# A hybrid convolution, expert and mLSTM block on one core: moving the column sums that open the convolution's layer norm further down TensorE's order

## The chip, the cores and the metric

The kernel runs on one core of a Trainium2 chip. The metric is the device time of one execution in microseconds (us), as the median of several runs. One execution was also taken with the hardware profiler; all rows below come from it.

## What is computed

The program is a first block (a convolution branch and a spatial gating branch, mixed by gates, then a mixture of 32 experts) followed by two layers of a second block. Only the convolution branch and what runs beside it matter here. For 512 tokens and 1024 channels, cut from the reference:

```python
def layer_norm(x, g, b):
    mu = jnp.mean(xf, axis=-1, keepdims=True)
    var = jnp.mean(jnp.square(xf - mu), axis=-1, keepdims=True)
    y = (xf - mu) * lax.rsqrt(var + EPS)
    return (y * g + b)
def conformer_conv_branch(a, conv_w, conv_b, ln_g, ln_b, w_o, b_o):
    a1, a2 = jnp.split(a, 2, axis=-1)
    a = a1 * jax.nn.sigmoid(a2)
    y = lax.conv_general_dilated(a, kern, ...) + conv_b     # 31 taps, depthwise
    y = jax.nn.silu(layer_norm(y, ln_g, ln_b))
    return y @ w_o + b_o
    ...
    g_a, g_b = jnp.split(jax.nn.sigmoid(gate_logits), 2, axis=-1)
    x = x + (g_a * y_a + g_b * y_b) @ w_out[l] + b_out[l]   # y_a convolution, y_b spatial gating
```

## The kernel before

Channels lie on the 128 partitions, tokens along the free axis, so a 1024 x 512 tensor is eight tiles of 128 x 512. A layer norm over channels needs sums across partitions. These are made on TensorE: `colsum` multiplies 128-token pieces of a tile by a column of ones (four instructions in the program, eight in the trace, since each float32 one runs as two), and `bcast_t` spreads a per-token number back over the partitions by four transposes (`bc` tiles).

Dense products run in three float16 products per 128 x 128 weight block (`mm3`): high part of the weights times high part of the data, high times low, low times high. One k-step below means these three matmuls of 128x512; an output tile (an `m`) takes eight k-steps and goes to one of eight PSUM tiles `p`. The weights come in chunks of 1 MB. A chunk is loaded into a `w` tile by a DMA from SP's queue, ScalarE makes the high half `wh` (L276), VectorE the low half `wl` (L280). A chunk of the products named below serves two output tiles.

The products of the first block run in this order on TensorE: `wa` (convolution input), `wv`, `wu`, `wgb`, `wga` (gates), `wsgo` (spatial gating output, data tiles `sh`), `wco` (convolution output, data tiles `ch`), `wo`, then routing and the experts.

Beside them the convolution runs in the background as `fillers`: the even channel tiles tap by tap on VectorE (L646), the odd ones as a scaled copy on ScalarE (`tap`, L628) and an add on GpSimd (L629). When a channel tile is whole, `conv_done` adds it to `ya` on GpSimd (L613, L615). With the last one it queues the norm's four steps: `ln_mu` (column sums `cs` of `ya`, mean `mu` on VectorE, L578), `ln_sub` (spread the mean, subtract it on VectorE, L587, squares on ScalarE, sums of squares `lsq` on VectorE, L465), `ln_r` (column sums of `lsq`, inverse root `rs`), `ln_out` (spread it, scale on VectorE, L602, SiLU and high half `ch` on ScalarE, L603 and L604, low half on VectorE, L606).

Every engine runs its own instructions in the order in which the program issued them. That order is set at build time by a clock of the builder, `self.clk`: each matmul adds its nominal length (0.213 us for a 128x512 one). `self.at(delay, fn)` puts a step into a heap with the due time `clk + delay`; `poll`, called after every k-step, issues the steps that are due. So a step lands behind a counted number of matmuls, whether or not its data are ready when the chip gets there, and each of the norm's steps queues the next by a delay of its own (3.0, 14.0 and 4.0).

Of the kernel before, what the change touches and what calls it, by code (L numbers as in the profile page):

```python
# [120 lines left out]
class Net:  # L121
# [385 lines left out]
    def first_mixer(self):  # L507
# [102 lines left out]
        def conv_done(m):  # L610
            whole.append(m)
            if len(whole) == 2:
                nc.gpsimd.tensor_add(ya, yc[whole[0]], yc[whole[1]])  # L613
            elif len(whole) > 2:
                nc.gpsimd.tensor_add(ya, ya, yc[m])  # L615
            if len(whole) == KD:
                self.at(5.0, ln_mu)

        def conv(m, ap):
            b = v("conv_b")[:, m:m + 1]  # L620
            yc[m] = self.t2([P, T], s="yc")
            if m % 2:
                y = yc[m]

                def tap(j):
                    q = self.tapp.tile([P, T], F32, name=self.name("tap"), tag="tap")
                    d = CONVW - 1 - j
                    nc.scalar.activation(q[:, d:T], ap[:, 0:T - d], AF.Copy, scale=cw[:, j, m:m + 1])  # L628
                    nc.gpsimd.tensor_add(y[:, d:T], y[:, d:T], q[:, d:T])  # L629
                    if j == 0:  # L630
                        conv_done(m)

                self.fillers[1].append(lambda: nc.scalar.activation(
                    y, ap, AF.Identity, scale=cw[:, CONVW - 1, m:m + 1], bias=b))
                for j in reversed(range(CONVW - 1)):
                    self.fillers[1].append(lambda j=j: tap(j))
                return
# [14 lines left out]
            def done():  # L652
                nc.scalar.activation(yc[m], y[0], AF.Copy)
                conv_done(m)
# [1101 lines left out]
```

## Time and profile before

| | |
|---|---|
| median of 3 runs | 1986.64 us (1985.33 to 1991.63) |
| the profiled execution | 1986.07 us |
| its span, first to last instruction | 1984.4 us |
| TensorE busy | 1923.0 us (97%) |
| VectorE, ScalarE, GpSimd busy | 989.8, 715.0, 239.4 us |
| mean granted TensorE clock | 0.989 |

Busy time counts instructions in flight, so a busy TensorE is not one at its peak, and its clock is granted in two levels, full (1.00, 2.4 GHz) and half (0.50, 1.2 GHz). What can be saved is seen where TensorE waits or runs at the lower level.

### The profile page before, as it was taken

How to read it: one execution, taken by the hardware profiler on the slowest of the kernel's cores; microseconds unless marked ns; L12 is line 12 of the kernel's file. 1: busy time of each engine (PE TensorE's matmuls, PEld its weight loads, DVE VectorE, ACT ScalarE, POOL GpSimd, SP SyncE). 2: the span in 40 equal slices, each digit the busy share in tenths (PEclk: the TensorE clock that was granted, in tenths of full speed). 3: DMA queues.
4: the chain of work that ended last, by engine and by line, in shares of the span. 5: the costliest groups of instructions: out<-in, count | busy, mean ns of one | idle time of the engine just before them, and what ended most of it. 6: DMA issues, size and time to landing. Idle time of an engine off the chain costs nothing.

```text
span 1984.4 us, 26464 instructions
## 1 busy us (share of the span) xinstructions
PE 1923.0 (97%) x10925; PEld 984.9 (50%) x10926; DVE 989.8 (50%) x1515; ACT 715.0 (36%) x1026; POOL 239.4 (12%) x194
## 2 busy tenths in 40 slices
PE   8999979989999999998999999999999999999997
PEld 3444434454434444433555864444485467444445
DVE  7888955642323323327645674423267558444223
ACT  6759643331111111115434564422143246443120
POOL 1998940010000000002000000000000000000000
PEclk9999989999999999998999999999999999999998
DMA  6333223369999999995421232322213322233201
GB/s 250 128 107 107 71 100 106 135 252 386 393 403 402 370 413 412 413 413 187 147 70 58 86 118 95 106 107 103 109 50 124 106 104 89 103 107 113 99 22 43
DMA packets 82476, 347.59 MB, mean 175 GB/s; under 512 B 9776, under 2 KB 12080, under 8 KB 57776
## 3 DMA queue, kind: packets, MB, share of 16 engines
q1 hardware_dynamic: 79776, 343.12, 46.4%
q10 hardware_dynamic: 2576, 2.74, 0.5%
q8 instruction: 87, 1.43, 0.3%
q14 instruction: 37, 0.30, 0.0%
HBM read 343.73 MB, written 2.10 MB: 174 GB/s over the span
## 4 chain that ended last, share of the span: by engine, by line
PE 58%; DMA 4%; DVE 3%; ACT 1%; issue 0%; POOL 0%; DVEq 0%; ACTq 0%; SPq 0%
PE p L182 48%; DMA ewl<-in_we_dram 3%; PE y L182 2%; PE pg L182 2%; PE pu L182 1%; PE sc L182 1%; PE xs L182 1%; DMA w<-in_we_dram 1%; DVE wl L280 1%; PE num L182 1%; DVE x L1266 1%; DVE d L1265 0%; PE bc L186 0%; DVE racc L465 0%; DVE xh L1234 0%
## 5 line engine op out<-in xcount | busy, mean ns | idle before, releaser
L182 PEld LDWEIGHTS <-wh 128*128 128x128 f16 x4448 | 436.3, 98 | 403.1 <-issue 9.1
L182 PE MATMUL p<-xh,wh 128*128 128x512 f16 (+1 forms) x1824 | 469.3, 347 | 3.4 <-ACT xh L1230 2.2
L280 DVE SCALAR_TENSOR_TENSOR wl<-w,wh 128x2048 f16<-128x2048 f32 x130 | 303.6, 2347 | 109.9 <-ACT wh L276 107.8
L182 PEld LDWEIGHTS <-wl 128*128 128x128 f16 x2224 | 218.2, 98 | 203.7 <-issue 4.6
L182 PE MATMUL p<-xh,wl 128*128 128x512 f16 (+1 forms) x912 | 316.7, 347 | 1.3 <-DVE wl L280 1.3
L182 PE MATMUL p<-hid,wh 128*128 128x512 f16 (+1 forms) x1152 | 308.8, 355 | 0.0
L276 ACT ACTIVATE wh<-w 128x2048 f16<-128x2048 f32 x130 | 244.9, 1902 | 6.1 <-PE p L182 3.8
L182 PE MATMUL p<-hid,wl 128*128 128x512 f16 (+1 forms) x576 | 204.7, 355 | 0.0
L629 POOL TENSOR_TENSOR yc<-yc,tap 128x511 f32<-128x511 f32 (+14 forms) x120 | 193.1, 1609 | 57.2 <-ACT tap L628 48.7
L182 PE MATMUL p<-hn,wh 128*128 128x512 f16 x576 | 173.0, 382 | 0.5 <-DVE hn L550 0.5
L465 DVE TENSOR_TENSOR pacc<-pacc,sq 128x256 f32<-128x256 f32 (+1 forms) x41 | 21.4, 522 | 208.3 <-ACT sq L464 208.2
L182 PE MATMUL p<-hn,wl 128*128 128x512 f16 x288 | 109.8, 381 | 0.0
L1610 DVE TENSOR_TENSOR relu<-relu 128x512 f32<-128x512 f32 (+1 forms) x76 | 46.1, 606 | 126.3 <-ACT hid L1609 126.3
L464 ACT ACTIVATE sq<-p 128x256 f32<-128x256 f32 (+1 forms) x41 | 18.9, 461 | 229.2 <-PE p L182 229.0
L1608 ACT ACTIVATE relu<-p 128x512 f32<-128x512 f32 (+1 forms) x76 | 39.9, 525 | 159.3 <-PE p L182 159.3
L646 DVE SCALAR_TENSOR_TENSOR yc<-ap,cw,yc 128x511 f32<-128x511 f32 (+14 forms) x120 | 88.3, 736 | 2.8
L1040 DVE TENSOR_TENSOR h<-h,pu 128x512 f32<-128x512 f32 x16 | 11.0, 688 | 154.3 <-PE pu L182 109.1
L628 ACT ACTIVATE tap<-ap,cw 128x511 f32<-128x511 f32 (+14 forms) x120 | 79.6, 701 | 22.0 <-POOL yc L629 21.9
L1039 ACT ACTIVATE h<-pg,wd 128x512 f32<-128x512 f32 x16 | 11.0, 687 | 195.3 <-PE pg L182 140.6
L182 PE MATMUL p<-wh,xh 128*128 128x512 f16 x256 | 79.7, 379 | 0.0
L1074 DVE TENSOR_TENSOR x<-x,sc 128x512 f32<-128x512 f32 x128 | 78.4, 681 | 1.6 <-PE sc L182 1.2
L1063 ACT ACTIVATE yhl<-y,wd 128x512 f16<-128x512 f32 x32 | 21.9, 687 | 144.4 <-PE y L182 116.5
(378 smaller groups left out, 2520.2 us busy)
## 6 DMA issues: line engine op xcount, KB each, us to landing
w<-in_wd_dram SPq DMA_DIRECT2D x130, 1024.0 KB, 4.9
w<-in_we_dram SPq DMA_DIRECT2D x62, 1024.0 KB, 12.6
ewh<-in_we_dram SPq DMA_DIRECT2D x90, 512.0 KB, 11.4
ewl<-in_we_dram SPq DMA_DIRECT2D x90, 512.0 KB, 10.2
ex<-in_we_dram SPq DMA_DIRECT2D x160, 256.0 KB, 5.3
x<-in_x_dram SPq DMA_DIRECT2D x8, 256.0 KB, 6.9
w<-in_wd_dram SPq DMA_DIRECT2D x4, 512.0 KB, 6.9
out_dram<-x ACTq DMA_DIRECT2D x8, 128.0 KB, 1.7
```

The lines of the kernel that those rows point to most:

```text
L182: self.nc.tensor.matmul(out, l, r, start=start, stop=stop)
L276: nc.scalar.activation(wh, t, AF.Copy, scale=WS)
L280: nc.vector.scalar_tensor_tensor(wl, t, WS, wh, op0=OP.mult, op1=OP.subtract)
L465: nc.vector.tensor_add(acc[:, s], acc[:, s], q)
L628: nc.scalar.activation(q[:, d:T], ap[:, 0:T - d], AF.Copy, scale=cw[:, j, m:m + 1])
L629: nc.gpsimd.tensor_add(y[:, d:T], y[:, d:T], q[:, d:T])
L646: V.scalar_tensor_tensor(y[0][:, d:T], ap[:, 0:T - d], cw[:, CONVW - 1 - d, m:m + 1], y[0][:, d:T], op0=OP.mult, op1=OP.add)
L1063: nc.scalar.activation(o[:, 0], y[q], AF.Copy, scale=wc)
L1074: V.tensor_add(xt[d], xt[d], ps)
L1266: (nc.gpsimd if i and last and k in (0, 2, 4) else nc.vector).tensor_add(x, x, d)
L1608: nc.scalar.activation(a, ps, AF.Relu, scale=IWS)
L1610: nc.vector.tensor_mul(a, a, a)
```

## The change

One number changes: the delay with which `conv_done` queues `ln_mu`.

```diff
             if len(whole) == KD:
-                self.at(5.0, ln_mu)
+                self.at(21.0, ln_mu)
```

Because the later steps of the norm are queued by their predecessors, they move along. No instruction is added or removed, and the numbers of instructions on all engines are the same.

TensorE, the place of the four `cs` sums that read `ya`. First the order before; the names are `p` for the output tile in PSUM, `hn` for the data of the gate products, `wh` and `wl` for the weights:

```order
L182 LDWEIGHTS wl_2013
L182 MATMUL p_2298<-hn_196,wl_2013 128x512
L182 MATMUL cs_2306<-ones_102,ya_211 128x1 x4
L182 LDWEIGHTS wh_2012
L182 MATMUL p_2298<-hn_197,wh_2012 128x512
```

They stood behind the second k-step of the sixth output tile of `wga`. The order of the change, with `sh` as the data of the spatial gating's output product:

```order
L182 LDWEIGHTS wl_2183
L182 MATMUL p_2385<-sh_1655,wl_2183 128x512
L182 MATMUL cs_2401<-ones_102,ya_211 128x1 x4
L182 LDWEIGHTS wh_2182
L182 MATMUL p_2385<-sh_1656,wh_2182 128x512
```

They now stand behind the third k-step of the first output tile of `wsgo`, that is 6 + 8 + 8 + 3 = 25 k-steps further down. The spreading of the mean follows 5 k-steps later in both, the sums of `lsq` after 22 k-steps more, the spreading of `rs` after 7 (before: 5 + 22 + 7 as well).

VectorE, between the last tap of the convolution (L646) and the first subtraction of the norm (L587). Before:

```order
L646 SCALAR_TENSOR_TENSOR yc_1826<-ap_854,cw_209,yc_1826 128x482
L280 SCALAR_TENSOR_TENSOR wl_2268<-w_400_1897,wh_2267 128x2048
L578 TENSOR_SCALAR mu_2305<-cs_2306 128x4
L587 TENSOR_TENSOR yc_405<-yc_405,bc_2327 128x512
L587 TENSOR_TENSOR yc_412<-yc_412,bc_2327 128x512
```

With the change:

```order
L646 SCALAR_TENSOR_TENSOR yc_1826<-ap_854,cw_209,yc_1826 128x482
L280 SCALAR_TENSOR_TENSOR wl_2268<-w_400_1897,wh_2267 128x2048
L280 SCALAR_TENSOR_TENSOR wl_2330<-w_427_2015,wh_2329 128x2048
L578 TENSOR_SCALAR mu_2400<-cs_2401 128x4
L280 SCALAR_TENSOR_TENSOR wl_2390<-w_441_2101,wh_2389 128x2048
L587 TENSOR_TENSOR yc_405<-yc_405,bc_2423 128x512
```

Two weight halves that stood behind the norm's subtractions now stand ahead of them, one of them ahead of the mean.

VectorE, between the last sum of squares (L465) and the first scaling of `ln_out` (L602). Before:

```order
L465 TENSOR_TENSOR lsq_2332<-lsq_2332,sq_2360 128x512
L280 SCALAR_TENSOR_TENSOR wl_2373<-w_427_2015,wh_2372 128x2048
L280 SCALAR_TENSOR_TENSOR wl_2433<-w_441_2101,wh_2432 128x2048
L436 TENSOR_SCALAR rsa_2455<-cs_2450 128x4
L442 TENSOR_TENSOR rsw_2457<-rsy_2456 128x4
L443 SCALAR_TENSOR_TENSOR rsw_2457<-rsw_2457,rsa_2455 128x4
L444 SCALAR_TENSOR_TENSOR rs_2458<-rsw_2457,rsy_2456 128x4
L773 SCALAR_TENSOR_TENSOR gate_1716<-p_2428,b_61_205,gate_1716 128x512
L602 TENSOR_TENSOR yc_405<-yc_405,bc_2495 128x512
```

With the change:

```order
L465 TENSOR_TENSOR lsq_2428<-lsq_2428,sq_2456 128x512
L773 SCALAR_TENSOR_TENSOR gate_1716<-p_2385,b_61_205,gate_1716 128x512
L773 SCALAR_TENSOR_TENSOR gate_1766<-p_2460,b_61_205,gate_1766 128x512
L280 SCALAR_TENSOR_TENSOR wl_2491<-w_455_2185,wh_2490 128x2048
L773 SCALAR_TENSOR_TENSOR gate_1835<-p_2486,b_61_205,gate_1835 128x512
L436 TENSOR_SCALAR rsa_2542<-cs_2537 128x4
L442 TENSOR_TENSOR rsw_2544<-rsy_2543 128x4
L443 SCALAR_TENSOR_TENSOR rsw_2544<-rsw_2544,rsa_2542 128x4
L444 SCALAR_TENSOR_TENSOR rs_2545<-rsw_2544,rsy_2543 128x4
L773 SCALAR_TENSOR_TENSOR gate_1884<-p_2518,b_61_205,gate_1884 128x512
L280 SCALAR_TENSOR_TENSOR wl_2563<-w_469_2270,wh_2562 128x2048
L602 TENSOR_TENSOR yc_405<-yc_405,bc_2588 128x512
```

Four evacuations of `wsgo` outputs (L773) and the two weight halves of the first `wco` chunks now lie between the two parts of the norm, where one evacuation and two `wsgo` weight halves lay.

## Rows read from the trace of the kernel before

**Rows 1.** The page: the span, busy time of each engine, and the span in 40 slices of 49.6 us (TensorE's busy tenths, its granted clock in tenths, GB/s moved by DMA).

```profile
span 1984.4 us, 26464 instructions
PE 1923.0 (97%) x10925; PEld 984.9 (50%) x10926; DVE 989.8 (50%) x1515; ACT 715.0 (36%) x1026; POOL 239.4 (12%) x194
...
PE   8999979989999999998999999999999999999997
...
PEclk9999989999999999998999999999999999999998
...
GB/s 250 128 107 107 71 100 106 135 252 386 393 403 402 370 413 412 413 413 187 147 70 58 86 118 95 106 107 103 109 50 124 106 104 89 103 107 113 99 22 43
```

**Rows 2.** TensorE's waits from 200 to 480 us, longest first: what waited, for whom, us in total, times, longest.

```profile
PE cs L182 <- POOL ya L615: 13.5, 1, 13.5
PE rk L182 <- DVE mk L933: 5.7, 1, 5.7
```

**Rows 3.** Stretches around that wait: us, busy time of each engine (instructions), granted clock, DMA share, GB/s.

```profile
250.00:255.00 5.00, 5.00 (x25) 2.25 (x23) 4.89 (x6) 2.31 (x4) 4.84 (x3) 1.00 0.22 49
...
256.00:270.00 14.00, 1.04 (x5) 1.04 (x6) 2.78 (x2) 4.05 (x5) 12.28 (x9) 0.67 0.28 101
270.00:272.00 2.00, 2.00 (x8) 1.17 (x9) 0.16 (x1) 0.00 (x0) 0.00 (x0) 0.50 0.00 0
272.00:276.00 4.00, 4.00 (x16) 1.72 (x15) 0.00 (x0) 0.00 (x0) 0.00 (x0) 0.70 0.00 0
276.00:280.00 4.00, 4.00 (x22) 1.93 (x20) 3.46 (x6) 2.07 (x4) 0.00 (x0) 1.00 0.00 0
```

**Rows 4.** TensorE in order of time around the wait: start, us from the start of the first to the end of the last, instruction, how many, idle time before and what ended it.

```profile
255.06 0.38 PE L182 MATMUL p<-hn,wl 128*128 128x512 f16 x1
268.96 1.87 PE L182 MATMUL cs<-ones,ya 128*128 128x1 f32 x8 [13.53 <-POOL ya L615]
270.69 1.01 PE L182 MATMUL p<-hn,wh 128*128 128x512 f16 x2
271.50 0.63 PE L182 MATMUL p<-hn,wl 128*128 128x512 f16 x1
...
274.06 0.55 PE L182 MATMUL p<-hn,wl 128*128 128x512 f16 x1
274.44 0.60 PE L182 MATMUL p<-hn,wh 128*128 128x512 f16 x2
...
275.52 0.38 PE L182 MATMUL p<-hn,wl 128*128 128x512 f16 x1
275.74 0.60 PE L186 MATMUL bc<-ident,mu 128*128 128x128 f32 x4
276.18 0.59 PE L182 MATMUL p<-hn,wh 128*128 128x512 f16 x2
```

**Rows 5.** TensorE in order of time where nothing holds it: the sums of `lsq`, the first matmuls behind the second spreading, and the first matmuls of `wco`.

```profile
290.21 0.38 PE L182 MATMUL p<-sh,wl 128*128 128x512 f16 x1
290.42 0.95 PE L182 MATMUL cs<-ones,lsq 128*128 128x1 f32 x8
291.23 0.38 PE L182 MATMUL p<-sh,wh 128*128 128x512 f16 x1
...
296.20 0.59 PE L182 MATMUL p<-sh,wh 128*128 128x512 f16 x2
...
329.87 0.59 PE L182 MATMUL p<-ch,wh 128*128 128x512 f16 x2
```

**Rows 6.** Who works during the wait. GpSimd's instructions by shape from 250 to 270 us (busy, mean ns), then in order of time the weight halves `wl` on VectorE, ScalarE's last instructions ahead of the norm, and GpSimd's last two adds.

```profile
L629 POOL TENSOR_TENSOR yc<-yc,tap 128x485 f32<-128x485 f32 x1 | 3.3, 3258 | 0.1
L629 POOL TENSOR_TENSOR yc<-yc,tap 128x490 f32<-128x490 f32 x1 | 3.2, 3153 | 0.1
...
L629 POOL TENSOR_TENSOR yc<-yc,tap 128x491 f32<-128x491 f32 x1 | 1.2, 1228 | 0.1
...
L629 POOL TENSOR_TENSOR yc<-yc,tap 128x484 f32<-128x484 f32 x1 | 1.2, 1202 | 0.1
...
250.02 2.78 DVE L280 SCALAR_TENSOR_TENSOR wl<-w,wh 128x2048 f16<-128x2048 f32 x1
259.04 2.29 DVE L280 SCALAR_TENSOR_TENSOR wl<-w,wh 128x2048 f16<-128x2048 f32 x1 [2.55 <-ACT wh L276]
...
257.11 1.89 ACT L276 ACTIVATE wh<-w 128x2048 f16<-128x2048 f32 x1
259.39 0.68 ACT L765 ACTIVATE gate<-p,cols 128x512 f32<-128x512 f32 x1
...
266.31 2.60 POOL L615 TENSOR_TENSOR ya<-ya,yc 128x512 f32<-128x512 f32 x2
```

**Rows 7.** VectorE in order of time through the norm: first subtraction, last sum of squares, the first of the inverse root, an evacuation of `wsgo`, first scaling, first and last low half of `ch`.

```profile
276.45 1.88 DVE L587 TENSOR_TENSOR yc<-yc,bc 128x512 f32<-128x512 f32 x3 [5.42 <-PE bc L186]
...
285.28 0.69 DVE L465 TENSOR_TENSOR lsq<-lsq,sq 128x512 f32<-128x512 f32 x1 [0.15 <-ACT sq L464]
...
292.82 0.15 DVE L436 TENSOR_SCALAR rsa<-cs 128x4 f32<-128x4 f32 x1
...
294.60 0.74 DVE L773 SCALAR_TENSOR_TENSOR gate<-p,b,gate 128x512 f32<-128x512 f32 x1
296.40 1.28 DVE L602 TENSOR_TENSOR yc<-yc,bc 128x512 f32<-128x512 f32 x2 [1.06 <-PE bc L186]
298.63 0.69 DVE L606 TENSOR_TENSOR ch<-yc,ch 128x512 f16<-128x512 f32 x1 [0.95 <-ACT ch L604]
...
308.50 0.69 DVE L606 TENSOR_TENSOR ch<-yc,ch 128x512 f16<-128x512 f32 x1 [0.68 <-ACT ch L604]
```

**Rows 8.** Behind the mixer: stretches as in rows 3 around the start of the experts and near their end, and TensorE's first expert matmuls.

```profile
420.00:430.00 10.00, 6.26 (x49) 5.08 (x48) 7.27 (x20) 6.45 (x13) 5.07 (x5) 1.00 0.65 263
430.00:440.00 10.00, 6.23 (x76) 6.03 (x78) 3.46 (x13) 1.88 (x2) 0.58 (x1) 0.66 0.01 2
440.00:450.00 10.00, 10.00 (x48) 3.31 (x46) 4.05 (x18) 1.80 (x4) 0.00 (x0) 1.00 0.70 257
...
800.00:900.00 100.00, 97.02 (x610) 41.07 (x608) 31.14 (x58) 12.53 (x20) 0.00 (x0) 1.00 1.02 413
...
439.78 1.08 PE L182 MATMUL pg<-w,xs 128*64 128x512 f32 x4
```

## The prediction

> **What bounds the kernel now.** I read the page first: TensorE is busy for 1923.0 of 1984.4 us, and the one slice of the mixer where both its busy share (7) and its granted clock (8) fall is the sixth, 248 to 298 us [rows 1]. The table of waits says why: one wait of 13.5 us of the sums `cs` for GpSimd's `ya`, the longest between 200 and 480 us, more than twice the next [rows 2]. The stretches show its second price: the clock is 0.67 on average from 256 to 270 us, 0.50 from 270 to 272, 0.70 from 272 to 276 and 1.00 afterwards [rows 3]. So TensorE comes back at half speed. The order of time gives the figures [rows 4]: a matmul starts at 255.06, then nothing until the sums at 268.96, and the matmuls behind them stand 0.43 us apart (270.69 to 271.50 for two) until 274.44, then 0.22. Meanwhile 25 k-steps of ready work stand behind the sums in TensorE's order, which nothing but the order holds back. GpSimd ends `ya` at 266.31 + 2.60 = 268.91 [rows 6]; it follows ScalarE's taps and VectorE, not TensorE.
>
> **What the change does to this wait.** First the pace. From 296.20 to 329.87 lie 52 k-steps (4 left of one `wsgo` output, six outputs of 8) with nothing between, 33.67 us [rows 5], so 0.6475 us each and 0.2158 per matmul. The sums without a wait push the next matmul from 290.21 + 0.22 to 291.23, 0.80 us; a spreading from 275.52 + 0.22 to 276.18, 0.44 us [rows 4, 5].
>
> In the new order the matmul behind 255.06 starts at 255.28. 25 k-steps take 16.19 us, so the sums are reached at 271.47, and their first weight load, which reads `ya`, at 271.26 (the sums stand 0.21 behind the last matmul's start [rows 5]). If `ya` is there, TensorE gains three terms:
> - the stall, from 255.28 to 268.96: 13.68 us;
> - the sums at the lower clock, 270.69 - 268.96 = 1.73 against 291.23 - 290.42 = 0.81: 0.92 us;
> - nine matmuls at the lower clock, 274.44 - 270.69 = 3.75 against 9 x 0.2158 = 1.94: 1.81 us.
>
> Together 16.4 us. The same from the other end: from 255.28 to the first matmul of `wco` are 86 k-steps (6 + 8 + 8 + 64), two sums and two spreadings, 55.69 + 1.60 + 0.88 = 58.2 us, so `wco` starts at 313.45 where it started at 329.87.
>
> **Is `ya` there?** This is the tight place. The work let through brings one new VectorE instruction in front of `mu`, `wl_2330`, and GpSimd slows beside such an instruction: the add of 128x485 took 3258 ns, its `wl` running from 259.04, where 128x484 took 1202; that of 128x490 took 3153 beside the `wl` from 250.02, where 128x491 took 1228 [rows 6]. That is 1.9 to 2.1 us per `wl`. When will it run? ScalarE is free at 259.39 + 0.6 = 260.0, does one gate then (its accumulator ends at 259.3) and the `wh` from about 260.6, 1.89 us; `wl_2330` runs from 262.5, in the middle of GpSimd's last taps. So `ya` ends at 268.91 + 2.0 = 270.9, at the latest bound of a whole `wl` (2.29) at 271.20, at the earliest at 268.91 if it falls between. All are before 271.26. I take no wait; the margin is 0.1 to 2.3 us, likeliest 0.3. The Trainium skill, "SBUF — State Buffer", section "Who interferes with whom", speaks against this margin: a VectorE instruction with two SBUF inputs and a GpSimd one that reads SBUF exclude each other, and whichever starts first holds the pair of ports for its whole length. By that rule the loss is the whole 2.29, the margin 0.06, and a handover would use it up; the slowed adds here lost slightly less than that.
>
> **What moves along, and why it costs nothing.** The rest of the norm hangs on TensorE's places, and these come out at the old times: spreading at 271.47 + 0.81 + 5 x 0.6475 = 275.52 (was 275.74), the sums of `lsq` at 290.2 (290.42), the second spreading at 295.6 (295.76). VectorE is ready for each. `wl_2390` waits for `wh_2389`, which follows the gate of the last `wga` output (ending at 269.7) on ScalarE and ends near 272.3, so it is done by 274.9, behind `mu` at 272.5, before the subtractions at 276.2. These run to 285.97 [rows 7]. Behind them queue evacuations and `wl_2491` (0.74 + 0.74 + 2.29 + 0.74 us): the inverse root starts near 291 instead of 292.82; an evacuation and `wl_2563` end by 296, where the scaling can start (296.40 before). So the first `ch` is whole at 299.3 and the last at 309.2, as before [rows 7]. `wco` needs the first at 313.45 and each next one 4 x 0.6475 = 2.6 us later, while they come 1.4 us apart: cover of 14.1 us, which was 30.5. The `wco` weights of the first two chunks are whole at 290 and 296, ahead of 313.45. The first `wsgo` accumulators stand full until VectorE comes to them at 286, four of the eight PSUM tiles at most; TensorE would stop only with eight. GpSimd's one instruction in the norm and SP's loads keep their order; a load waits for the `wl` that frees its tile, and none of those moves behind the matmul that needs the chunk.
>
> **Does the gain survive the experts?** From 440 us on the weights' stream runs at a DMA share of 1.0 (413 GB/s at 800 to 900 us), so this stage could take back what the mixer gives. But its loads stop for want of free tiles: 263 GB/s at 420 to 430, 2 GB/s at 430 to 440, and go on when TensorE uses the first expert weights from 439.78 [rows 8]. The stream's restart hangs on TensorE and moves with it. Even if all the loading ahead stayed at its old time, there are 10 us of rest; at most 16.4 - 10 = 6.4 us would be lost.
>
> **Sum.** The profiled execution took 1986.07 us (span 1984.4), 0.57 under the median of the runs shown. 1986.07 - 16.42 = 1969.65; with half of that 0.57 as the median's due I say 1969.9 us.
>
> **The rivals.**
> - *The sums still wait for `ya`.* For it: the margin of 0.1 to 0.3. Against: every row gives an end before 271.26. The rule above speaks for it too. If one more `wl` length (2.0) fell in, the wait is 1.7: 1971.6. If TensorE's clock fell again, add up to 0.92 + 1.81: 1974.3. The wait of 5.7 us for `mk` lies in the stretch where the clock shows 0.66, so a wait under 2 us may cost the clock or not [rows 2, 8].
> - *The experts give part back.* The loads ahead stay, up to 6.4 us lost: 1972 to 1976. Against: the rest at 430 to 440.
> - *The gain is lost whole, or the change does nothing.* The `wco` product or the experts wait for what TensorE no longer waits for: 1981 to 1988. The order shows that the sums do move past 16.2 us of work, so it must come from a wait behind.
> - *Slower: `wco` waits for `ch`.* VectorE runs in order, and `rsa`, which opens the inverse root, now stands behind three evacuations and `wl_2491`, which waits for ScalarE's `wh_2490`. If that chain slips, `ch` slips one for one. TensorE begins to pay when the first `ch` comes 14.1 us late, and the kernel is slower than before only when it comes over 14.1 + 16.4 = 30.5 us late: a slip of 35 us gives 1991. Nothing on these queues is longer than 2.3 us.
>
> **How the numbers follow.** Forecast 0.76 (own range 1968 to 1971.5), the sums wait 0.10, the experts give back 0.07, the gain lost 0.04, slower 0.03. The first three are all more than 0.3% (6 us, about what a measurement of this kernel can tell from no change) below the median. Faster 0.93, same 0.04, slower 0.03. The low end is 1969.65 less the 1.3 by which the lowest run lay under the median and 1 us for the terms' own error: 1967.3. The high end takes in the waiting sums and most of the experts' share: 1975.
>
> **What would show it.** Right: no wait of `cs` for `ya` in the table, or one under 0.5 us; a clock of 1.00 from 250 to 320 us; the first matmul on `ch` near 313.5 with no wait, the last `ch` near 309; GpSimd's last add ending near 271; the first expert matmul near 423.4; DMA still at rest just ahead of it. Wrong: a wait of `cs` over 1 us, a new wait at the head of `wco`, or expert waits for DMA that grow by more than 2 us in sum.

## The result and the profile after

The changed kernel takes 1970.36 us (median of 4 runs, 1969.88 to 1971.26), the kernel before 1988.18 us on the same footing (4 runs, 1985.33 to 1991.63). The ratio is 0.991, with a 95% interval of 0.9897 to 0.9923: faster by 0.9%. The forecast was 1969.9 us.

The profiled execution of the change took 1970.78 us. Its page, as in rows 1 (span, busy times, TensorE's busy tenths and granted clock in 40 slices):

```profile
span 1969.1 us, 26465 instructions
PE 1921.1 (98%) x10925; PEld 985.3 (50%) x10926; DVE 991.9 (50%) x1515; ACT 715.0 (36%) x1026; POOL 240.7 (12%) x194
...
PE   8999999989999999998999999999999999999997
...
PEclk9999999999999999998999999999999999999998
```

The 7 and the 8 in the sixth slice [rows 1] are nines now. TensorE's busy time fell by 1.9 us only, while the span fell by 15.3: what went is time in which it did nothing, and the little that fell is the work that ran at half speed. The table of its waits from 200 to 460 us, longest first, begins with what stood second in rows 2:

```profile
PE rk L182 <- DVE mk L933: 5.7, 1, 5.7
PE xs L182 <- DVE oh L947: 1.2, 1, 1.2
PE y L182 <- ACT hT L1048: 0.7, 1, 0.7
PE cs L182 <- ACT sq L847: 0.7, 1, 0.7
```

No wait of `cs` for `ya` is left, and no new one has come. The stretches that answer to rows 3 (busy time of TensorE, weight loads, VectorE, ScalarE, GpSimd, then granted clock, DMA share, GB/s):

```profile
255.00:270.00 15.00, 15.00 (x72) 6.81 (x70) 6.33 (x4) 7.96 (x9) 14.37 (x9) 1.00 0.51 185
270.00:272.00 2.00, 2.00 (x11) 0.92 (x10) 0.00 (x0) 1.42 (x2) 0.61 (x1) 1.00 0.00 0
272.00:276.00 4.00, 4.00 (x25) 2.33 (x23) 2.37 (x2) 1.07 (x1) 0.00 (x0) 1.00 0.00 0
```

TensorE is busy throughout and the clock stays at its full level, where it was 0.67, 0.50 and 0.70. TensorE in order of time, for rows 4 and 5: the matmul behind which the sums used to stand, the sums at their new place, and the first matmuls of `wco`:

```profile
255.92 0.38 PE L182 MATMUL p<-hn,wl 128*128 128x512 f16 x1
...
272.11 0.38 PE L182 MATMUL p<-sh,wl 128*128 128x512 f16 x1
272.33 0.95 PE L182 MATMUL cs<-ones,ya 128*128 128x1 f32 x8
...
314.31 0.59 PE L182 MATMUL p<-ch,wh 128*128 128x512 f16 x2
```

From the first of these rows to `wco` are 58.4 us; in rows 4 and 5 it was 329.87 - 255.06 = 74.8. The difference is 16.4 us, the sum that the prediction made. But the first row itself stands 0.86 us later than 255.06, and this comes from the start of the program. There, in the first product, TensorE runs at half pace until the clock rises; the row at which its matmuls become 0.22 us apart is this one in the execution before:

```profile
11.38 0.47 PE L182 MATMUL p<-xg,wl 128*128 128x512 f16 x1
11.69 0.60 PE L182 MATMUL p<-xg,wh 128*128 128x512 f16 x2
```

and this one in the execution of the change:

```profile
12.80 0.57 PE L182 MATMUL p<-xg,wl 128*128 128x512 f16 x1
13.21 0.59 PE L182 MATMUL p<-xg,wh 128*128 128x512 f16 x2
```

Nothing there was changed. By the same reading the other executions below went over between 11.0 and 13.9 us. So the two spans differ by 15.3 and not by 16.4: 0.86 us is luck of the start, and 0.2 us is spread over the rest.

### The profile page after: what moved, and what is told of

It is laid out like the page before. It is cut to its first block, busy times and chain, and to the rows that moved or that the text cites. A ratio compares the mean times of both kernels' runs of the same rounds, so it can differ in the third digit from the quotient of the medians.

```text
span 1969.1 us, 26465 instructions
## 1 busy us (share of the span) xinstructions
PE 1921.1 (98%) x10925; PEld 985.3 (50%) x10926; DVE 991.9 (50%) x1515; ACT 715.0 (36%) x1026; POOL 240.7 (12%) x194
## 4 chain that ended last, share of the span: by engine, by line
PE 54%; DMA 8%; DVE 3%; ACT 1%; issue 1%; POOL 0%; SPq 0%; DVEq 0%; ACTq 0%
PE p L182 48%; DMA ewl<-in_we_dram 5%; DMA w<-in_we_dram 3%; PE y L182 1%; PE sc L182 1%; DVE wl L280 1%; PE num L182 1%; PE xs L182 1%; PE pg L182 1%; DVE x L1266 1%; PE pu L182 0%; DVE d L1265 0%; PE bc L186 0%; DVE racc L465 0%; DVE xh L1234 0%
## 5 line engine op out<-in xcount | busy, mean ns | idle before, releaser
L465 DVE TENSOR_TENSOR pacc<-pacc,sq 128x256 f32<-128x256 f32 (+1 forms) x41 | 21.4, 521 | 208.4 <-ACT sq L464 208.3
L646 DVE SCALAR_TENSOR_TENSOR yc<-ap,cw,yc 128x511 f32<-128x511 f32 (+14 forms) x120 | 88.3, 736 | 2.8
```

The lines of the kernel that those rows point to most:

```text
L465: nc.vector.tensor_add(acc[:, s], acc[:, s], q)
L646: V.scalar_tensor_tensor(y[0][:, d:T], ap[:, 0:T - d], cw[:, CONVW - 1 - d, m:m + 1], y[0][:, d:T], op0=OP.mult, op1=OP.add)
```

## The experiments

The theory under test is that of the prediction: the whole gain is one stall of TensorE on `ya` and the half-speed clock behind it, bought out of cover that the norm had ahead of `wco`. The first four runs change the one number to other values, so each run moves the same step to another place; they share the runs of the kernel before, 1989.47 us in that comparison.

**Half of the move.**

```diff
-                self.at(21.0, ln_mu)
+                self.at(13.0, ln_mu)
```

> The sums are queued 8 builder's us later instead of 16, so 39 matmuls (8.4 us) of ready work go ahead of them instead of 75. My theory (the gain is the covered stall plus the half-speed clock behind it): TensorE reaches the sums near 263.7 to 264.6 us, ya ends near 270.6 as in the changed kernel, so 6.0 to 6.9 us of the wait stay; if a wait of that length costs the clock, up to 2.7 us more. 1976.4 to 1980. Rival (the place of the sums matters for something else, such as the order of VectorE's weight halves, and not for the wait): about 1970, as the full change, or 1988, as before.

It took 1981.65 us (ratio to the kernel before 0.9964, 0.9952 to 0.9975). TensorE in order of time:

```profile
263.06 0.38 PE L182 MATMUL p<-hn,wl 128*128 128x512 f16 x1
271.15 1.87 PE L182 MATMUL cs<-ones,ya 128*128 128x1 f32 x8 [7.71 <-POOL ya L615]
272.88 1.01 PE L182 MATMUL p<-hn,wh 128*128 128x512 f16 x2
```

The sums are reached at 263.4 and wait 7.7 us, so a part of the move gives a part of the gain and the place alone does nothing: the rival is out. The clock fell in full: the sums take 1.73 us and the next matmuls stand 0.43 us apart, as in rows 4. The time is 1.7 us above my upper end. The wait accounts for 0.8 us of this, since `ya` ends at 271.1 in this execution, not at 270.6, and TensorE comes to the sums 0.3 us before the earliest time that I had; the rest is not taken apart here.

**Three quarters of the move.**

```diff
-                self.at(21.0, ln_mu)
+                self.at(17.0, ln_mu)
```

> 57 matmuls (12.3 us) go ahead of the sums, which TensorE reaches near 267.6 to 268.5 us: a wait of 2.2 to 3.0 us for ya stays. If a wait this short keeps the clock at full speed: 1972.6 to 1973.4. If the clock falls as after the long wait: up to 2.7 us more, 1976. This prices the rival of the prediction in which the sums still wait for a short time.

It took 1975.20 us (1972.64 to 1976.88; ratio 0.9936, 0.9919 to 0.9952). The median lies nearer to the 1976 of the case in which the clock falls than to 1972.6 to 1973.4. In the profiled execution, of 1972.64 us, `ya` ended at 269.0 and the wait was short. TensorE in order of time, then two stretches of one us each with their clock:

```profile
269.02 1.05 PE L182 MATMUL cs<-ones,ya 128*128 128x1 f32 x8 [1.64 <-POOL ya L615]
269.93 0.75 PE L182 MATMUL p<-hn,wh 128*128 128x512 f16 x2
...
273.46 0.69 PE L182 MATMUL p<-sh,wh 128*128 128x512 f16 x2
```

```profile
271.00:272.00 1.00, 1.00 (x4) 0.35 (x3) 0.00 (x0) 0.00 (x0) 0.00 (x0) 0.50 0.06 16
272.00:273.00 1.00, 1.00 (x3) 0.30 (x2) 0.00 (x0) 0.00 (x0) 0.00 (x0) 0.50 0.00 0
```

A wait of 1.64 us already brings the half level, although the sums right behind it still ran at their full pace (0.91 us). Nine matmuls take 273.46 - 269.93 = 3.53 us instead of 1.94. So a short wait costs nearly as much in clock (1.6 us) as in waiting. This is the price of the rival in which the sums still wait; the 21 of the change is just beyond it.

**Further than the change.**

```diff
-                self.at(21.0, ln_mu)
+                self.at(33.0, ln_mu)
```

> The sums go 28.5 us further down than before the change, 12.3 us further than in the changed kernel, so the whole norm is later by 12.3 us: first ch near 312, last near 322, while wco starts near 314.3 and takes one more ch every 2.6 us. My theory (cover of 14.1 us at the head of wco): nothing is lost, 1970.4 within 1 us, and no wait on ch. Rival (the cover is smaller than the rows say, since evacuations and weight halves on VectorE push the norm): a wait at the head of wco, one us of time per us, 1972 to 1980.

It took 1969.87 us (ratio 0.9912, 0.9896 to 0.9929), the same as the change. The head of `wco`, in TensorE's order of time, shows no gap although the first `ch` became whole only at about 311:

```profile
312.95 0.38 PE L182 MATMUL p<-sh,wl 128*128 128x512 f16 x1
313.16 0.59 PE L182 MATMUL p<-ch,wh 128*128 128x512 f16 x2
```

So 12.3 us of the cover can be spent for nothing, and the change is on a plateau, not at a best point. No wait of the norm's sums or spreadings shows in its trace, so the edge of the cover is not seen in this run.

**Beyond the cover.**

```diff
-                self.at(21.0, ln_mu)
+                self.at(45.0, ln_mu)
```

> Beyond the cover: the sums of lsq and the second spreading now stand at the head of wco (the heap is emptied there), with the inverse root and the first scaling, SiLU and cast between them and the first ch. By the rows of the norm TensorE waits about 2.2 us for rs and 2.4 to 3.2 us for ch: 1970.4 + 4.6 to 5.4 = 1975 to 1975.8, and up to 2.7 us more if the clock falls. Rival (the wait at wco is hidden by work elsewhere, for instance taken up by the experts' loads): 1970 to 1972.

It took 1980.50 us (ratio 0.9958, 0.9942 to 0.9975): 10 us of the gain are gone. TensorE at the head of `wco`, and the stretch behind it:

```profile
312.83 0.95 PE L182 MATMUL cs<-ones,lsq 128*128 128x1 f32 x8
317.52 1.11 PE L186 MATMUL bc<-ident,rs 128*128 128x128 f32 x4 [3.74 <-DVE rs L444]
320.93 1.31 PE L182 MATMUL p<-ch,wh 128*128 128x512 f16 x2 [2.29 <-ACT ch L604]
```

```profile
320.00:326.00 6.00, 4.93 (x12) 1.65 (x12) 4.76 (x8) 5.84 (x10) 0.00 (x0) 0.50 0.00 0
```

Both waits are where the theory puts them, 6.0 us together; that for `rs` is 1.5 us longer than I had it, most of the 2.0 us by which the time lies above my upper end (1975.8 + 2.7 = 1978.5). The product then starts at a clock of 0.50: its matmuls reach from 320.9 to 365.0, 44.1 us, where they took 41.0 in the change. The first expert matmul is 9.8 us later than in the change and the end 9.7 us: the experts take up nothing of it. This is the slower rival of the prediction, made to happen; the order of the change stands 24 of the builder's us away from it.

The next three share other runs of the kernel before, 1987.58 us.

**The clock alone.** The kernel before, with dummy work ahead of the sums:

```diff
             mu = self.sm([P, NT], s="mu")
+            keep, fill = self.clk, self.ps(s="fill")
+            for j in range(60):
+                self.mm(fill, self.ones16, hn[0][:, 0], j == 0, j == 59)
+            self.clk = keep
             nc.vector.tensor_scalar(mu, self.colsum(ya), 1.0 / D, None, op0=OP.mult)
```

> The kernel before with 60 extra float16 matmuls of 128x512 (12.9 us) ahead of the sums, into a PSUM tile that nobody reads; the order of everything else is as before. The wait for ya is still there, but TensorE is busy during it. My theory (2.7 us of the 16.4 are the clock, 0.9 in the sums and 1.8 in the matmuls behind them): the sums start near 269 as before, at a granted clock of 1.00, and the time falls by 2.7 us against the kernel before. Rival (the clock costs nothing beyond the wait): same as before; or the extra matmuls outlast the wait: up to 0.5 us slower.

It took 1985.89 us; the ratio of 0.9991 (0.9981 to 1.0002) does not tell it from the kernel before. The trace does show the term. TensorE in order of time:

```profile
269.47 1.05 PE L182 MATMUL cs<-ones,ya 128*128 128x1 f32 x8 [0.52 <-POOL ya L619]
270.38 0.59 PE L182 MATMUL p<-hn,wh 128*128 128x512 f16 x2
270.81 0.38 PE L182 MATMUL p<-hn,wl 128*128 128x512 f16 x1
```

The sums take 0.91 us and the matmuls stand 0.22 us apart at once. From the start of the sums to `wco` are 327.74 - 269.47 = 58.3 us against 329.87 - 268.96 = 60.9 [rows 4, 5]: 2.6 us, where I had worked out 2.7. Half of it is not seen at the end: the span is 1983.0 us, 1.4 less than that of the execution before. `ya`, and with it the sums, come 0.5 us later in this execution, and 0.7 us is lost behind the first expert matmul, around a branch that TensorE takes in the middle of the experts (L1091, a step for overfull experts that is skipped here). The branch instruction of TensorE's queue (count, ns min/median/max, start in us) in the change and in this run, where the line number is larger by the four lines added:

```profile
L1091 PEldq COMPARE_BRANCH  x1: 445/445/445, 648.5 to 648.5; - x1
```

```profile
L1095 PEldq COMPARE_BRANCH  x1: 6009/6009/6009, 661.9 to 661.9; - x1
```

Behind it the next expert matmul waits 2.6 us instead of 0.5, and the granted clock is 0.57 from 668 to 672 us. This costs more than the 0.7 us at first; the rest is made up later among the experts. So the term is shown where it arises, and its worth in the time of the whole kernel is not.

**The cause taken away instead of the order.** The kernel before with `ya` early. This leaves out 11 of the 31 taps of one channel tile and 8 of another:

```diff
                 def tap(j):
+                    if m == 7 and 1 <= j <= 11:
+                        return
...
             def tap0(d):
+                if m == 6 and d > 22:
+                    return
```

> The order of the kernel before, but with ya ready early: the last channel tile of GpSimd's share leaves out 11 of its 31 taps and the last of VectorE's share 8 of 31, so this computes a shorter convolution for two of eight channel tiles. TensorE's order is untouched. My theory (the wait is for ya alone): ya ends near 256 to 258 us, the wait shrinks to at most 2.5 us, and the time is that of the changed kernel, 1970 to 1973. Rival (TensorE would find another wait there, such as weights or PSUM, and it is the order itself that helps): 1980 to 1988.

It took 1970.92 us (median of 5; 0.9926, 0.9902 to 0.9950), as the change does, in the old order. GpSimd's last adds and TensorE's sums:

```profile
252.51 4.53 POOL L615 TENSOR_TENSOR ya<-ya,yc 128x512 f32<-128x512 f32 x2
```

```profile
257.10 1.05 PE L182 MATMUL cs<-ones,ya 128*128 128x1 f32 x8 [0.86 <-POOL ya L615]
258.02 0.59 PE L182 MATMUL p<-hn,wh 128*128 128x512 f16 x2
258.45 0.38 PE L182 MATMUL p<-hn,wl 128*128 128x512 f16 x1
```

Where `ya` is there, the old place costs little: the wait is 0.86 us, and from the matmul ahead of the sums (255.87) to `wco` (315.38) are 59.5 us, against 74.8 in the kernel before and 58.4 in the change. The wait for `ya` is the whole cause, and the order of VectorE's weight halves, which this run leaves as it was, has no part in it. It also shows a wait of 0.86 us behind which the clock did not fall.

**The same clock term at another wait.** The changed kernel, with more of its dummy matmuls ahead of `rk`:

```diff
-    LATE, IDLE = 5, 7
+    LATE, IDLE = 5, 31
```

> The changed kernel with 31 instead of 7 of its dummy matmuls ahead of the rank sums rk in the routing, where TensorE waits 5.7 us for mk and then runs at a lower clock. 24 more matmuls are 5.2 us, inside that wait. If what the clock costs behind the sums holds there too, the 64 gather matmuls xs take about 3.7 us instead of 5.6 and the expert weights are asked for 2 us earlier: 1968.4, if the experts pass it on (the loads rest ahead of it for 8 us). Rival (the experts' weight stream takes it back): 1970.4. Other rival (the dummy matmuls end later than mk): up to 1 us slower.

It took 1972.84 us (0.9923, 0.9903 to 0.9944), 2.5 us over the change: a miss. TensorE in order of time, and three stretches with their clock:

```profile
417.24 0.19 PE L182 MATMUL rk<-mk,tri 128*128 128x32 f16 x1 [0.49 <-DVE mk L933]
418.85 5.36 PE L182 MATMUL xs<-oh,hmt 128*128 128x128 f16 x64 [1.20 <-DVE oh L947]
```

```profile
410.00:417.00 7.00, 6.75 (x32) 2.84 (x29) 6.48 (x16) 3.41 (x7) 5.24 (x5) 1.00 0.12 48
417.00:419.00 2.00, 0.57 (x13) 0.50 (x14) 1.35 (x4) 0.00 (x0) 0.00 (x0) 1.00 0.00 0
419.00:423.00 4.00, 4.00 (x49) 4.00 (x47) 0.00 (x0) 1.49 (x2) 0.00 (x0) 0.62 0.02 4
```

The wait for `mk` was filled (0.49 us, was 5.7) and the clock was full through it. It fell all the same behind the next 1.6 us, in which TensorE had ten small matmuls and a wait of 1.2 us. The gather took 5.36 us (5.68 in the change), not 3.7. And with the 48 added instructions the branch took 5987 ns, with a wait of 2.6 us behind it.

**The branch.** Two looks at what makes it slow: 8 dummy matmuls more than the change has, and 6 fewer (`IDLE` of 15 and of 1).

> The changed kernel with 15 instead of 7 dummy matmuls ahead of rk: 16 more TensorE instructions (a weight load and a matmul each), all inside the wait for mk. In the two kernels with 48 and 120 more instructions ahead of it, TensorE's branch at L1091 took 6.0 us instead of 0.45 and held the next expert matmul 2.6 us instead of 0.5. If any added instruction does that: a branch of 6 us here too and 1972.5. If it hangs on how many are added: 0.45 us and 1970.4.

> The changed kernel with 1 instead of 7 dummy matmuls ahead of rk: 12 TensorE instructions fewer. If the branch at L1091 is slow only when instructions are added: 0.45 us, and a wait of 0.5 us behind it. If the number decides in either direction: 6 us and 2.6 us may show here as well. The wait for mk grows by the 1.3 us that the dummies took and nothing else changes: 1970 to 1973 with a spread of 2 us for a single run.

With 16 instructions more the branch of the profiled execution took 445 ns, with 12 fewer 1145 ns. But the length of this record does not tell what it costs. The first expert matmul behind the branch, first with 16 more and then with 12 fewer, and a stretch with 16 more:

```profile
653.83 1.01 PE L182 MATMUL pg<-ewh,xs 128*64 128x512 f32 x1 [2.51 <-DVEq L1091]
```

```profile
652.41 0.61 PE L182 MATMUL pg<-ewh,xs 128*64 128x512 f32 x1 [0.48 <-PEq L1091]
```

```profile
653.00:657.00 4.00, 3.17 (x8) 1.31 (x9) 0.69 (x1) 0.00 (x0) 0.00 (x0) 0.57 0.99 406
```

So neither case came out as stated: with 16 more the branch is short and the wait behind it is there all the same, 2.51 us, with the lower clock behind it, as with 48 and 120 more. All three kernels with added instructions have this wait; the eight others have 0.5 us. Why is not shown. What differs in the traces is the place of the 16 KiB packets of the instruction queue q8: the last one ahead of the branch started 1.3 to 2.3 us before it in the eight kernels and 4.0 to 6.6 us before it in the three, which points to the fetching of instructions and does not show it. The times (1972.97 us, 1970.79 to 1974.87 in four runs, and 1970.88 us in one) do not tell either from the change.

## Why the prediction was right

**The stall, 13.7 us, and the clock, 0.9 + 1.8 us.** All three terms are gone from the trace of the change, and 16.4 us is what lies between the two kernels from the old place of the sums to `wco`. The runs price them apart: the filled wait gives 2.6 us for the clock between the sums and `wco`, and the run with an early `ya` gives the whole gain without moving anything.

**Whether `ya` is there.** The margin was the tight step. The one GpSimd add in the change that is slow and was not in rows 6, then the new weight half on VectorE, and GpSimd's end, for rows 6:

```profile
L629 POOL TENSOR_TENSOR yc<-yc,tap 128x483 f32<-128x483 f32 x1 | 3.1, 3131 | 0.1
...
262.74 2.84 DVE L280 SCALAR_TENSOR_TENSOR wl<-w,wh 128x2048 f16<-128x2048 f32 x1 [1.67 <-ACT wh L276]
...
268.00 2.61 POOL L615 TENSOR_TENSOR ya<-ya,yc 128x512 f32<-128x512 f32 x2
```

`wl_2330` ran at 262.74 (I had 262.5) and cost one more add its 1.9 us, as its fellows in rows 6. `ya` ended at 270.61 (I had 270.9), 1.5 us ahead of the first weight load of the sums. Of this 0.86 is the late start of TensorE, and 0.26 is that GpSimd's adds stand earlier here (from 243.26 us, in the execution before from 243.52); 0.4 is left, near the 0.3 that I called likeliest. That `wl` took 2.84 us itself where one alone takes 2.29: it began while an add was running. The Trainium skill's rule ("SBUF — State Buffer", "Who interferes with whom"), that the one which starts first keeps the other out, agrees with both rows; the add loses 1.9 us and not the whole length of the `wl`, as it began (263.52) when 2.07 us of the `wl` were left. Five more runs have the same order up to this place. In the three with other numbers of dummy matmuls the margin was 1.9 to 2.0 us; in those at 33 and 45, whose sums stand further down, it would have been 0.2 us (`ya` ended at 270.76 and 271.73, and the matmul that would have been the last ahead of the sums started at 270.96 and 271.88). So the margin moves by 2 us between executions, and it can be as thin as I feared.

**The norm keeps its times, and the cover holds.** VectorE in the change, for rows 7: first subtraction, inverse root, first scaling, first and last low half of `ch`:

```profile
277.08 1.88 DVE L587 TENSOR_TENSOR yc<-yc,bc 128x512 f32<-128x512 f32 x3 [1.40 <-PE bc L186]
...
292.04 0.16 DVE L436 TENSOR_SCALAR rsa<-cs 128x4 f32<-128x4 f32 x1 [1.27 <-PE cs L182]
...
297.03 1.28 DVE L602 TENSOR_TENSOR yc<-yc,bc 128x512 f32<-128x512 f32 x2 [0.27 <-PE bc L186]
299.26 0.69 DVE L606 TENSOR_TENSOR ch<-yc,ch 128x512 f16<-128x512 f32 x1 [0.94 <-ACT ch L604]
...
309.17 0.69 DVE L606 TENSOR_TENSOR ch<-yc,ch 128x512 f16<-128x512 f32 x1 [0.72 <-ACT ch L604]
```

With the 0.86 us of the start taken off they stand where the prediction put them, and each of the first three waits for TensorE, so nothing that was moved ahead on VectorE holds the norm up. The first `ch` is whole at 299.95, 14.4 us ahead of `wco` (I had 14.1). The runs at 33 and 45 bracket that figure: 12.3 us later costs nothing, 24 us later costs 10.

**The experts pass it on.** The first expert matmul, and the stretch ahead of it, for rows 8:

```profile
414.00:424.00 10.00, 5.79 (x71) 5.72 (x72) 3.82 (x13) 1.72 (x2) 1.02 (x1) 0.66 0.01 2
...
424.27 1.08 PE L182 MATMUL pg<-w,xs 128*64 128x512 f32 x4
```

It starts 15.5 us earlier than in rows 8, the loads rest ahead of it as before, and TensorE's waits for expert weights (`w` and `ewl`) are 2.8 and 0.6 us in all in both kernels.

**What was off.** The spread of the start, up to 2.8 us between the earliest and the latest rise of the clock in these executions, did not stand in the range. That the median of the change fell within 0.5 us of the forecast is in part luck. All terms were read from one execution of the kernel before, of 1986.07 us, while the median of that kernel moved from 1986.64 to 1988.18 with one more run and was 1987.58 to 1989.47 beside the experiments. Between the medians the change is worth 17.8 us, 1.4 more than the sum; where that difference lies, no trace here shows.

## What to carry to other kernels

A wait in front of a small instruction on an in-order engine is bought back by counting the ready work behind it: move the instruction down by at least the wait, check what comes to run beside its producer there, and check the cover of everything that hangs on it. Then the exact place does not matter (21 and 33 gave the same), but half a move gives less than half the gain, since what is left of the wait can still bring the lower clock: the 7.7 us did, and the 1.64 us too, while the 0.86 us with the early `ya` did not. Filling a wait with dummy work to keep the clock up has to be judged on the whole program: here it bought 2.6 us at its place, and the whole time (1985.89 against 1987.58 us) does not tell it from no change.

## What the runs showed of the hardware that was not expected

- A wait of 1.64 us, with the 0.9 us of small sums behind it, was followed by a granted clock of 0.50; one of 0.86 us with the same sums was not, and 31 large matmuls right ahead of 1.6 us of small ones and waiting did not keep the clock from 0.62 behind them.
- TensorE's taken branch took 0.35 to 1.1 us in nine of the eleven kernels and 6.0 us in the two with 48 and 120 instructions more ahead of it. The expert matmul behind it waited 2.5 to 2.6 us in these two and in the kernel with 16 more, whose branch took 0.45 us, and 0.5 us in the eight others. The cause is not shown.
- The first rise of the clock came between 11.0 and 13.9 us in executions whose program is the same up to there.
